# Top-2 gate dispatch: the first 14-row store waits for the landing of a 30-row load

## The chip, the cores and the metric

One core of one Trainium2 chip runs the kernel. The time is device microseconds of one execution, given as the median of several. The kernel before takes 240.29 us (three runs, 240.19 to 240.34).

## The reference

`x` holds 16 x 1024 tokens of 512 float32 values, `router_logits` 8 logits for each token, and k is 2.

```python
probs = softmax(router_logits)                      # over the 8 experts
topk_indices = np.argsort(probs, axis=-1)[..., -k:]
topk_probs = np.take_along_axis(probs, topk_indices, axis=-1)
topk_probs = topk_probs / np.sum(topk_probs, axis=-1, keepdims=True)
x_expanded = x[:, :, np.newaxis, :].repeat(k, axis=2)
return (x_expanded * topk_probs[..., np.newaxis]).astype(np.float32)
```

So each token is written out twice, scaled by the smaller and by the larger of its two normalized top-2 weights. With two weights the softmax cancels: they are the sigmoid of minus and plus the difference of the two largest logits. The kernel reads 33.6 MB of `x`, half a MB of logits, and writes 67.1 MB.

## The kernel before

**Layout.** The 16,384 tokens are dealt out in two groups (`GROUPS`, line 49): 128 partitions times 65 tokens, then 128 times 63. A "row" below is one token in each of the 128 partitions: 256 KB to load, 512 KB to store. `xs` holds the input rows of one group (65 rows), `osp` 16 rows of output. Within a partition the rows of one load or store are contiguous in HBM, so a load of 32 rows moves 128 pieces of 64 KB.

**Loads.** The loop at line 111 issues the loads of a group on SP's queue in the sizes of `LOADS` (line 51): 2, 4, 2, 8, 17 and 32 rows for the first group, 16, 16 and 31 for the second. After the second load the two loads of logits are issued (lines 116 and 117), and `top2_weights` finds the two largest logits of each token in a tournament on VectorE (lines 27 to 40), and on ScalarE two sigmoids (lines 42 and 43), which give `WA`.

**Products and stores.** `plan` (lines 120 to 126) lists the stretches of a group in order: first row, number of rows, place of the output. For the first group: 2 rows and 14 rows into `osp`; 16 rows into `xs[0:32]`, over input rows already used; 8 and 8 rows into the two halves of `osp`; then 9 and 8 rows over `xs[31:65]`. For the second group: 16 rows into `osp`, 16 over `xs`, 8 and 8 into `osp`, 15 over `xs`. `over` (line 98) finds the place in `xs`. For each stretch one multiplication on VectorE (line 128) writes both scaled copies, and one store follows (line 136), on ACT's queue for the 2-row stretch (`n == e`) and on SP's for all others.

**Order.** There is one core and no hand-written schedule: each engine takes its instructions in program order, and waits on semaphores where a tile is still to be read or written. SP issues all loads of the first group, then its stores, then the loads of the second group, each when the rows of `xs` it overwrites have been stored, then the stores of the second group. A store into `osp` must have landed before VectorE writes that part of `osp` again. Transfers complete on eight semaphores used in turn, and an issue that takes a semaphore again waits for the transfer that used it before.

The change touches the list of sizes (line 51), the loop of loads (lines 110 to 113) and the store (lines 135 and 136). The store it makes wait is the one with `g == 0` and `r == e`, which is the first group's second stretch: 14 rows from `osp`, 7168 KB, the first store on SP's queue.

Of the kernel before, what the change touches and what calls it, by code (L numbers as in the profile page):

```python
# [1 line left out]

# [4 lines left out]

F32 = mybir.dt.float32
ALU = mybir.AluOpType
ACTF = mybir.ActivationFunctionType  # L10
P = 128


def top2_weights(nc, pool, logits, M, E, tag=""):

    hi, lo, n = None, None, E  # L20
    while n > 1:
        n //= 2
        if hi is None:
            a, b = logits[:, :, 0:n], logits[:, :, n : 2 * n]
            nhi = pool.tile([P, M, n], F32, tag=f"hi{n}{tag}")
            nlo = b
            nc.vector.tensor_tensor(nhi, a, b, op=ALU.max)  # L27
            nc.vector.tensor_tensor(nlo, a, b, op=ALU.min)  # L28
        else:
            a, b = hi[:, :, 0:n], hi[:, :, n : 2 * n]  # L30
            nhi = pool.tile([P, M, n], F32, tag=f"hi{n}{tag}")
            nlo = pool.tile([P, M, n], F32, tag=f"lo{n}{tag}")
            tmp = pool.tile([P, M, n], F32, tag=f"tmp{n}{tag}")
            nc.vector.tensor_tensor(tmp, lo[:, :, 0:n], lo[:, :, n : 2 * n], op=ALU.max)  # L34
            nc.vector.tensor_tensor(nlo, a, b, op=ALU.min)  # L35
            nc.vector.tensor_tensor(nlo, nlo, tmp, op=ALU.max)  # L36
            nc.vector.tensor_tensor(nhi, a, b, op=ALU.max)  # L37
        hi, lo = nhi, nlo
    dlt = pool.tile([P, M], F32, tag=f"dlt{tag}")
    nc.vector.tensor_tensor(dlt, hi[:, :, 0], lo[:, :, 0], op=ALU.subtract)  # L40
    WA = pool.tile([P, M, 2], F32, tag=f"WA{tag}")
    nc.scalar.activation(WA[:, :, 0], dlt, ACTF.Sigmoid, scale=-1.0)  # L42
    nc.scalar.activation(WA[:, :, 1], dlt, ACTF.Sigmoid, scale=1.0)  # L43
    return WA

GROUPS = [65, 63]

LOADS = [[2, 4, 2, 8, 17, 32], [16, 16, 31]]


LAST = [[(48, 9), (57, 8)], [(48, 15)]]


@with_exitstack
def kernel(
    ctx: ExitStack,
    tc: tile.TileContext,  # L60
    x: bass.AP,
    router_logits: bass.AP,
    k: bass.AP,
    out: bass.AP,
):
    nc = tc.nc
    B, S, D = x.shape
    E = router_logits.shape[-1]
    N = B * S
    assert int(k) == 2 and E == 8 and N == P * sum(GROUPS)  # L70
    M = N // P

    L = 16
    x_v, o_v, rl_v = [], [], []
    t0 = 0
    for n in GROUPS:
        t1 = t0 + P * n
        x_v.append(
            x.rearrange("b s d -> (b s) d")[t0:t1].rearrange("(p m) d -> p m d", p=P)
        )  # L80
        o_v.append(
            out.rearrange("b s k d -> (b s) k d")[t0:t1].rearrange(
                "(p m) k d -> p m k d", p=P
            )
        )
        rl_v.append(
            router_logits.rearrange("b s e -> (b s) e")[t0:t1].rearrange(
                "(p m) e -> p m e", p=P
            )
        )  # L90
        t0 = t1

    wpool = ctx.enter_context(tc.tile_pool(name="wpool", bufs=1))
    logits = wpool.tile([P, M, E], F32)
    xs = wpool.tile([P, max(GROUPS), D], F32)
    osp = wpool.tile([P, L, 2, D], F32)

    def over(r, n, G):

        a = 2 * r - G
        return xs[:, a : a + 2 * n, :].rearrange("p (r k) d -> p r k d", k=2)

    h = L // 2
    e = 2
    m0 = 0
    for g, G in enumerate(GROUPS):
        r = 0  # L110
        for n in LOADS[g]:
            nc.sync.dma_start(xs[:, r : r + n, :], x_v[g][:, r : r + n, :])  # L112
            r += n
            if g == 0 and r == 6:

                nc.sync.dma_start(logits[:, :G], rl_v[0])  # L116
                nc.sync.dma_start(logits[:, G:], rl_v[1])
                WA = top2_weights(nc, wpool, logits, M, E)
        assert r == G
        begin = [(0, e, osp[:, :e]), (e, L - e, osp[:, e:])] if g == 0 else [(0, L, osp)]  # L120
        plan = begin + [
            (L, L, over(L, L, 2 * L)),
            (2 * L, h, osp[:, :h]),
            (2 * L + h, h, osp[:, h:]),
        ]
        plan += [(r, n, over(r, n, G)) for r, n in LAST[g]]
        for r, n, og in plan:
            nc.vector.tensor_tensor(  # L128
                og,
                xs[:, r : r + n, :].unsqueeze(2).to_broadcast([P, n, 2, D]),  # L130
                WA[:, m0 + r : m0 + r + n, :].unsqueeze(3).to_broadcast([P, n, 2, D]),
                op=ALU.mult,
            )

            queue = nc.scalar if n == e else nc.sync
            queue.dma_start(o_v[g][:, r : r + n], og)  # L136
        m0 += G


# [1 line left out]
_INS = ['x', 'router_logits', 'k']  # L141
_OUTS = [((16, 1024, 2, 512), 'float32')]

_NUMBERS = {'k': 2}


# [26 lines left out]
```

## Time and profile before

| what | us |
|---|---|
| median of three runs | 240.29 |
| span of the profiled execution, first to last instruction | 238.5 |
| VectorE busy | 142.0 |
| ScalarE busy | 1.8 |

SP's issues and VectorE's products, from the timeline (the start, then the length; a transfer's length here is that of the issue alone):

| start us | engine | what |
|---|---|---|
| 0.73 to 4.8 | SP | loads of 2, 4 rows, logits, loads of 2, 8, 17, 32 rows |
| 12.75 to 30.06 | VectorE | products of 2 and 14 rows |
| 15.08 | ACT | store of 2 rows |
| 30.07 | SP | store of 14 rows |
| 30.08 to 47.32 | VectorE | product of 16 rows, over `xs` |
| 47.33 | SP | store of 16 rows |
| 64.02 | VectorE | products of 8 and 8 rows, after 16.71 us of waiting |
| 102.30, 113.52, 123.48 | SP | loads of the second group |
| 214.42 | SP | last store |

The page's times are of one execution under the profiler. "q1" is SP's queue of transfers and "q10" ACT's; both are served by 16 DMA engines. A row of the view by windows gives the stretch, its length, the busy time of DVE, ACT and POOL in it with the number of instructions, the granted TensorE clock, the busy share of the DMA engines and their rate in GB/s. A landing time counts from the issue of a transfer to its completion. A strip of 40 numbers gives the rate in 40 equal slices, each packet booked in the slice in which it starts.

### The profile page before, as it was taken

To read this page: it belongs to the slowest core of one execution; us is meant where nothing else is said; L and a number is where in the kernel's file an instruction comes from. 1 tells how busy PE (TensorE), PEld (TensorE's weight loads), DVE (VectorE), ACT (ScalarE), POOL (GpSimd) and SP (SyncE) were. 2 spreads that over 40 slices of the span, in tenths; PEclk is the share of its full clock that TensorE was granted. 3 is DMA by queue.
4 is the path that set the end of the run, shared out by engine and by line. 5 is a ranking of instruction groups with operands and counts; after the bars stand their busy time and mean duration, and the time that the engine had idled before them with its cause. 6 is when DMAs were issued, how large, how long until landed. Compare 5 with 4: busy or idle time off the path is not lost.

```text
span 238.5 us, 116 instructions
## 1 busy us (share of the span) xinstructions
DVE 142.0 (60%) x23; ACT 1.8 (1%) x3; POOL 0.2 (0%) x4
## 2 busy tenths in 40 slices
DVE  0599999900299699900000699999006999990000
ACT  2000000000000000000000000000000000000000
POOL 0000000000000000000000000000000000000000
DMA  7999989899898999999999999998999989999994
GB/s 261 434 470 411 459 383 528 330 462 462 352 506 352 440 440 440 440 414 465 440 429 434 412 478 458 394 495 374 462 418 429 451 363 429 440 440 429 495 453 206
DMA packets 3312, 101.19 MB, mean 424 GB/s; under 512 B 368, under 2 KB 496, under 8 KB 880
## 3 DMA queue, kind: packets, MB, share of 16 engines
q1 hardware_dynamic: 3168, 100.14, 97.8%
q10 hardware_dynamic: 144, 1.05, 1.0%
HBM read 34.08 MB, written 67.11 MB: 424 GB/s over the span
## 4 chain that ended last, share of the span: by engine, by line
DMA 43%; DVE 41%; issue 4%; SPq 1%; ACT 0%; DVEq 0%
DVE xs L128 22%; DVE osp L128 18%; DMA out_dram<-xs 15%; DMA xs<-in_x_dram 13%; DMA out_dram<-osp 13%; DMA logits<-in_router_logits_dram 3%; SPq L112 0%; DVE nhi L27 0%; DVE logits L28 0%; DVE nlo L36 0%; DVE nhi L37 0%; DVE tmp L34 0%; DVE nlo L35 0%; SPq L116 0%; SPq L136 0%
## 5 line engine op out<-in xcount | busy, mean ns | idle before, releaser
L128 DVE TENSOR_TENSOR osp<-xs,WA 128x8192 f32<-128x8192 f32 (+3 forms) x7 | 69.1, 9908 | 61.9 <-DMA xs<-in_x_dram 31.2
L128 DVE TENSOR_TENSOR xs<-xs,WA 128x16384 f32<-128x16384 f32 (+3 forms) x5 | 69.1, 13812 | 2.2 <-DMA out_dram<-xs 2.0
L27 DVE TENSOR_TENSOR nhi<-logits 128x512 f32<-128x512 f32 x1 | 0.7, 691 | 8.3 <-DMA logits<-in_router_logits_dram 8.3
L42 ACT ACT_TABLE_LOAD x1 | 1.3, 1283 | 0.7 <-PEq L154 0.7
L28 DVE TENSOR_TENSOR logits<-logits 128x512 f32<-128x512 f32 x1 | 0.7, 692 | 0.0
L37 DVE TENSOR_TENSOR nhi<-nhi 128x256 f32<-128x256 f32 (+1 forms) x2 | 0.7, 351 | 0.0
L35 DVE TENSOR_TENSOR nlo<-nhi 128x256 f32<-128x256 f32 (+1 forms) x2 | 0.7, 350 | 0.0
L36 DVE TENSOR_TENSOR nlo<-nlo,tmp 128x256 f32<-128x256 f32 (+1 forms) x2 | 0.7, 350 | 0.0
L34 DVE TENSOR_TENSOR tmp<-logits 128x256 f32<-128x256 f32 x1 | 0.4, 418 | 0.0
L42 ACT ACTIVATE WA<-dlt 128x128 f32<-128x128 f32 x1 | 0.3, 315 | 10.2 <-DVE dlt L40 10.2
L40 DVE TENSOR_TENSOR dlt<-nhi,nlo 128x128 f32<-128x128 f32 x1 | 0.3, 291 | 0.0
L43 ACT ACTIVATE WA<-dlt 128x128 f32<-128x128 f32 x1 | 0.3, 297 | 0.0
L34 DVE TENSOR_TENSOR tmp<-nlo 128x128 f32<-128x128 f32 x1 | 0.3, 283 | 0.0
L154 POOL MEMSET const-bfloat16-1.0<- 128x1 bf16 x1 | 0.1, 101 | 0.0
L154 POOL MEMSET const-uint8-127<- 128x1 uint8 x1 | 0.1, 101 | 0.0
L154 POOL MEMSET const-float32-0.0<- 128x1 f32 x1 | 0.1, 98 | 0.2 <-issue 0.2
L154 POOL MEMSET const-float32-1.0<- 128x1 f32 x1 | 0.1, 98 | 0.0
## 6 DMA issues: line engine op xcount, KB each, us to landing
out_dram<-osp SPq DMA_DIRECT2D x4, 4096.0 KB, 20.7
xs<-in_x_dram SPq DMA_DIRECT2D x2, 4096.0 KB, 29.9
xs<-in_x_dram SPq DMA_DIRECT2D x1, 7936.0 KB, 38.0
out_dram<-xs SPq DMA_DIRECT2D x1, 7680.0 KB, 23.2
out_dram<-osp SPq DMA_DIRECT2D x1, 7168.0 KB, 33.9
out_dram<-xs SPq DMA_DIRECT2D x1, 4608.0 KB, 20.4
xs<-in_x_dram SPq DMA_DIRECT2D x1, 4352.0 KB, 22.4
out_dram<-xs SPq DMA_DIRECT2D x1, 4096.0 KB, 21.5
```

The lines of the kernel that those rows point to most:

```text
L27: nc.vector.tensor_tensor(nhi, a, b, op=ALU.max)
L28: nc.vector.tensor_tensor(nlo, a, b, op=ALU.min)
L34: nc.vector.tensor_tensor(tmp, lo[:, :, 0:n], lo[:, :, n : 2 * n], op=ALU.max)
L35: nc.vector.tensor_tensor(nlo, a, b, op=ALU.min)
L36: nc.vector.tensor_tensor(nlo, nlo, tmp, op=ALU.max)
L37: nc.vector.tensor_tensor(nhi, a, b, op=ALU.max)
L40: nc.vector.tensor_tensor(dlt, hi[:, :, 0], lo[:, :, 0], op=ALU.subtract)
L42: nc.scalar.activation(WA[:, :, 0], dlt, ACTF.Sigmoid, scale=-1.0)
L43: nc.scalar.activation(WA[:, :, 1], dlt, ACTF.Sigmoid, scale=1.0)
L128: nc.vector.tensor_tensor(og, xs[:, r : r + n, :].unsqueeze(2).to_broadcast([P, n, 2, D]), WA[:, m0 + r : m0 + r + n, :].unsqueeze(3).to_b ...
L154: nc = _bacc.Bacc("TRN2", target_bir_lowering=False, num_devices=1)
```

## The change

The first group's load of 32 rows is issued as two, of 30 rows and 2 rows. Loads and stores are kept in program order, and the first group's store of 14 rows gets a dependency on the second-last load, the one of 30 rows: SP issues it only once that load has landed, as well as the product of its rows. At that time only the load of 2 rows is ahead of it in the queue. SP's order of issue is otherwise the same; the computation and all other transfers are the same.

```diff
-LOADS = [[2, 4, 2, 8, 17, 32], [16, 16, 31]]
+LOADS = [[2, 4, 2, 8, 17, 30, 2], [16, 16, 31]]
...
-        r = 0
+        r, loads = 0, []
         for n in LOADS[g]:
-            nc.sync.dma_start(xs[:, r : r + n, :], x_v[g][:, r : r + n, :])
+            load = nc.sync.dma_start(xs[:, r : r + n, :], x_v[g][:, r : r + n, :])
+            loads.append(tc.keep_in_program_order(load))
             r += n
...
             queue = nc.scalar if n == e else nc.sync
-            queue.dma_start(o_v[g][:, r : r + n], og)
+            store = tc.keep_in_program_order(queue.dma_start(o_v[g][:, r : r + n], og))
+            if g == 0 and r == e:
+
+                tc.add_manual_dep(
+                    store.ins,
+                    loads[-2].ins.name,
+                    mybir.DependencyInfo(
+                        mybir.DependencyClass.Sync, mybir.DependencyReason.DATA
+                    ),
+                    reason="store behind the loads",
+                )
```

## The prediction

> **What bounds the kernel now.** I read the page first: is any engine or transfer the limit over the whole span? The answer is the transfers.
>
> ```profile
> span 238.5 us, 116 instructions
> DVE 142.0 (60%) x23; ACT 1.8 (1%) x3; POOL 0.2 (0%) x4
> q1 hardware_dynamic: 3168, 100.14, 97.8%
> HBM read 34.08 MB, written 67.11 MB: 424 GB/s over the span
> ```
>
> Packets of SP's queue alone (q1) fill 97.8% of the time of 16 DMA engines; VectorE (DVE) works 60%. So the chain of waits, which names DVE for 41%, only passes through work that lies beside transfers. A change pays, or costs, what it takes from or adds to the time in which the DMA engines stand still or run slowly. I therefore cut the span at the places where the kind of transfer changes, and read the rate of each stretch (the last column, GB/s; the column before is the busy share of the DMA engines).
>
> ```profile
> 0.00:1.74 1.74, 0.00 (x0) 1.01 (x1) 0.20 (x4) 1.00 0.00 0
> 1.74:4.00 2.26, 0.00 (x0) 0.27 (x1) 0.00 (x0) 1.00 1.02 330
> 33.56:43.22 9.66, 9.66 (x1) 0.00 (x0) 0.00 (x0) 1.00 1.00 434
> 43.22:46.19 2.97, 2.97 (x1) 0.00 (x0) 0.00 (x0) 1.00 1.03 353
> 46.19:63.10 16.91, 1.12 (x1) 0.00 (x0) 0.00 (x0) 1.00 1.00 434
> 63.10:82.42 19.32, 17.29 (x2) 0.00 (x0) 0.00 (x0) 1.00 1.00 434
> 82.42:112.67 30.25, 18.45 (x2) 0.00 (x0) 0.00 (x0) 1.00 1.00 433
> 112.67:141.71 29.04, 8.68 (x1) 0.00 (x0) 0.00 (x0) 1.00 1.00 433
> 141.71:160.44 18.73, 18.70 (x2) 0.00 (x0) 0.00 (x0) 1.00 1.01 434
> 160.44:218.44 58.00, 40.52 (x4) 0.00 (x0) 0.00 (x0) 1.00 1.00 434
> 218.44:236.56 18.12, 0.00 (x0) 0.00 (x0) 0.00 (x0) 1.00 1.00 434
> ```
>
> From 46.19 us to the end every stretch runs at 433 to 434 GB/s. So there is no slack behind the changed store: whatever it is late by is late at the end, one for one. One stretch is slow: 43.22 to 46.19 us, where the last eighth of the 32-row load goes through and the first big store begins. Slices of 0.1 us from 43 to 47 us show the starts of these packets:
>
> ```profile
> GB/s 0 0 4588 1966 2621 1311 0 0 0 0 0 0 0 0 0 0 0 0 0 0 0 0 0 0 0 0 0 0 0 0 0 573 1147 2294 2294 1720 1147 0 0 0
> ```
>
> A packet is booked where it starts. The last wave of the load starts between 43.2 and 43.6, the first wave of the store between 46.2 and 46.7 (the earliest at 46.19): 2.97 apart, where four earlier waves took 9.66 us, 2.42 each. The junction from load to store costs 0.55 us. The next such junction, at 160.44, shows nothing (434).
>
> Two more views give the instants of the issues and landings:
>
> ```profile
> 30.07 0.35 SPq L136 DMA_DIRECT2D out_dram<-osp  x1
> 47.33 0.34 SPq L136 DMA_DIRECT2D out_dram<-xs  x1
> ...
> xs<-in_x_dram SPq DMA_DIRECT2D x1, 42.6
> out_dram<-osp SPq DMA_DIRECT2D x1, 7168.0 KB, 33.9
> ```
>
> The store of 14 rows is issued at 30.07, 16 us before its first packet: it sits in the queue behind the load. The 32-row load is issued at 4.4 (two issues of 0.45 and 0.41 us from 3.85), so it lands at 47.0, 0.35 us after its last packet gives way to the store's.
>
> **The change, part by part.**
>
> *Two loads for one.* The bytes stay. One issue more on SP (0.4 us) falls before 8 us, when SP has nothing to issue until 30.07: hidden; uncovered it would cost its 0.4. It also waits for the landing of the 4-row load (the same semaphore is reused), at 6.9, long before its own bytes are due near 44.8. The short rows go in packets of 4 KB; the stretch 4.00 to 8.00, full of packets of 2 to 8 KB, still ran at 405 GB/s, so 0.52 MB cost 1.29 instead of 1.21 us: +0.08, beside the wait below, so 0 in the sum and +0.08 where the wait vanishes.
>
> *The wait.* Without the slow junction the 32 rows would end at 45.6 to 46.0 (43.2 to 43.6 plus 2.42). Two rows are 1.21 us at 433 GB/s, so the 30-row load ends at 44.4 to 44.8 and lands at 45.15 (plus the 0.35 above). SP then issues; take 0.05, since the second group's second load was issued at 113.52 when the 4608 KB store whose rows it overwrites landed (93.15 + 20.4 = 113.55): no delay to be seen. From issue to the first packet: the row is the kernel's first load, issued at 0.73, nothing moving before 1.74, its 16 first packets starting from 1.74 to 2.05: 1.01 to 1.32. So the store starts at 46.2 to 46.5, middle 46.36; before it was 46.2 to 46.7, middle 46.45. Difference -0.09.
>
> *The refill.* After an emptied queue the rate is not full at once: 1.74 to 4.00 moved 0.746 MB, which is 1.72 us at 433, in 2.26. Of the 0.54 lost, 0.15 is the mean of the spread of starts, counted already; 0.39 is the upper bound (those were small reads from HBM, this is a large write), 0 the lower. I take half, +0.2.
>
> *Sum:* 238.5 - 0.09 + 0.2 = 238.6 of span; the median 240.29 lies 1.8 above the profiled span, which stays: 240.4.
>
> *What the wait holds back.* Behind the store on SP is the 16-row store, which needs DVE until 47.33; the wait ends at about 45.2, so 2.1 us of cover are left; only an issue after 47.33 would move it. ACT and DVE wait for nothing new: DVE's next product (64.02) waits for the same store's landing and moves with it. Its cover further on is ample: at 214.42 the last store is issued 4 us before its packets are due at 218.44.
>
> *Bounds of the unknown.* The time from issue to first packet behind two moving rows has no row of its own. Least: 0.35, the issue instruction itself (then the two rows' end decides). Most: the 2-row store on ACT's queue was issued at 15.08, and the queue's first packets stand in the stretch from 18 to 19 us,
>
> ```profile
> q10 hardware_dynamic: 7, 0.06, 13.5%
> ```
>
> from about 18.6 on: 3.5 us after the issue, among long packets of the other queue. I take 1.01, the row of the same queue with nothing ahead; the two small rows are nearer to that than to a queue with packets of 34 KB.
>
> A rule of the Trainium skill speaks against the change (DMA: Bandwidth & Descriptors, "Anatomy of one DMA"): any wait happens on the issuing sequencer, engines just consume what is queued, and each DMA has about 2 us fixed, mostly the confirmation of the last byte. By that figure 2.0 less the 1.21 of the two rows would be a gap of 0.8, and after the 0.55 of the junction +0.25: 240.5. The trace's own 0.35 and 1.01 make 1.4.
>
> **Rivals.**
>
> *Faster: the store follows the two rows without a gap and the slow junction is gone.* Gain 0.55 less 0.08: -0.47, 239.8. For it: the load lands 1.2 us before the queue is empty. Against: it needs 0.5 us or less from issue to packet, half of what the one clean row has. Even this is the whole of it, because nothing else in the trace is slow after 46.19.
>
> *Slower: the junction's 0.55 belongs to the first big store on SP's queue, not to its having been queued behind a load.* Then it is paid after the gap as well: +0.11 + 0.55 = +0.66, 240.95. For it: the second junction, load to store in the same manner, cost nothing, so queueing alone does not make it. Against: the stretched packets are the load's, not the store's. It decides if the time from issue to first packet is 1.5 us or more, or if the store's first wave is longer than 2.1 us.
>
> *Slower: generation of the packets is late beside moving data,* towards ACT's row: halfway between 1.01 and 3.54 is 2.28, +1.27 on the forecast, 241.7; it decides above 1.4 us.
>
> *The change does nothing:* the load would have to land before 30.07; the 42.6 us exclude it.
>
> **How the numbers follow.** What a measurement of this kernel tells from no change is about 0.2%, 0.48 us. Forecast 240.4, its own range 240.05 to 240.75 (the refill from 0 to 0.39, 0.15 for the landing): 47%. Faster rival 13%, of which half may reach past 239.8 by some relief I don't see. First-store rival 22%, late generation 18%. So faster 0.13, same 0.47, slower 0.40. The range takes in the faster rival's time and the lower half of late generation: 239.7 to 241.5.
>
> **What would show it.** In the changed profile: the 30-row load lands at 45.0 to 45.4; SP's first big store is issued within 0.1 us of that; no packet starts for some 0.3 to 0.6 us before the store's first wave at 46.2 to 46.6; the last wave of the 30-row load lasts 2.27, not 2.8. If the DVE product that began at 64.02 begins at 64.0 to 64.3, the sum holds; at 63.6 the faster rival is right, from 64.6 on a slower one. The prediction is wrong, too, if later stretches drop below 433 GB/s, that is, if the order on the 16 DMA engines matters beyond this junction.

## The result, and the profile after

The changed kernel takes 241.98 us (five runs, 241.97 to 242.1) against 240.29: a ratio of 1.0069, 95% interval 1.0057 to 1.008. It is 0.7% slower; 240.4 was forecast, in a range up to 241.5.

The page after, in the same lines as before: the engines do the same work, the bytes are the same, and the span has grown by 1.8 us.

```profile
span 240.3 us, 116 instructions
DVE 142.0 (59%) x23; ACT 1.8 (1%) x3; POOL 0.2 (0%) x4
q1 hardware_dynamic: 3312, 100.14, 97.7%
HBM read 34.08 MB, written 67.11 MB: 421 GB/s over the span
```

Did the wait do what was said? SP's issues and landing times, and the starts of packets in slices of 0.1 us from 43 to 47 us:

```profile
45.36 0.35 SPq L137 DMA_DIRECT2D out_dram<-osp  x1
47.40 0.34 SPq L137 DMA_DIRECT2D out_dram<-xs  x1
...
xs<-in_x_dram SPq DMA_DIRECT2D x1, 7680.0 KB, 40.9
out_dram<-osp SPq DMA_DIRECT2D x1, 7168.0 KB, 18.3
...
GB/s 0 0 0 0 0 0 0 0 0 0 0 0 0 0 205 164 410 451 328 532 410 369 451 410 369 532 246 246 82 41 0 0 6881 2294 0 0 0 0 0 0
```

It did. The load of 30 rows lands at 45.3 (issued at 4.44), the store is issued at 45.36 instead of 30.07, the two small rows run from 44.4 to 46.0, two slices are empty, and the first packets of the store stand in two slices, 46.2 to 46.4, where before they were spread over six. No packet is stretched at this junction any more. The next product on VectorE begins earlier than before, at 63.78 instead of 64.02. But the lines after it, VectorE's products of the changed kernel, tell of a loss:

```profile
63.78 17.29 DVE L129 TENSOR_TENSOR osp<-xs,WA 128x8192 f32<-128x8192 f32 x2 [16.40 <-DMA out_dram<-osp]
83.21 18.48 DVE L129 TENSOR_TENSOR xs<-xs,WA 128x9216 f32<-128x9216 f32 x2 [2.14 <-DMA out_dram<-xs]
134.00 17.23 DVE L129 TENSOR_TENSOR osp<-xs,WA 128x16384 f32<-128x16384 f32 x1 [32.30 <-DMA xs<-in_x_dram]
```

Before, these began at 64.02, 83.36 and 133.03: the changed kernel is 0.24 ahead, then 0.15 ahead, then 0.97 behind. By its last store (issued at 216.33 instead of 214.42) it is 1.9 behind. The windows of the changed kernel, cut where waves of packets begin (a wave is one packet on each of the 16 engines), show where:

```profile
44.44:46.21 1.77, 1.77 (x1) 0.00 (x0) 0.00 (x0) 1.00 0.74 296
46.21:63.21 17.00, 1.17 (x1) 0.00 (x0) 0.00 (x0) 1.00 1.02 439
63.21:82.59 19.38, 17.29 (x2) 0.00 (x0) 0.00 (x0) 1.00 0.99 426
82.59:112.98 30.39, 18.45 (x2) 0.00 (x0) 0.00 (x0) 1.00 1.00 431
...
121.50:123.29 1.79, 0.00 (x0) 0.00 (x0) 0.00 (x0) 1.00 0.96 256
...
159.12:162.42 3.30, 3.30 (x1) 0.00 (x0) 0.00 (x0) 1.00 1.06 328
162.42:220.41 57.99, 39.52 (x4) 0.00 (x0) 0.00 (x0) 1.00 1.00 433
```

Two views of the kernel before, for comparison: the starts of packets from 118 to 126 us, where the waves follow each other every 1.2 us, and the window of the load wave near 160 us.

```profile
GB/s 0 0 0 492 983 1147 0 0 0 492 819 1311 0 0 0 328 983 1311 0 0 0 328 983 1147 164 0 0 328 819 1147 328 0 0 328 819 1147 328 0 0 328
...
158.08:160.44 2.36, 2.36 (x1) 0.00 (x0) 0.00 (x0) 1.00 1.03 430
```

The three store windows up to 112.98 and that of 159.12 hold the same packets as their counterparts in the kernel before, so lengths can be compared. The three store stretches up to 112.98 take 17.00, 19.38 and 30.39 instead of 16.91, 19.32 and 30.25: 0.3 us more in all. Then two windows stand out, and they are the two places where the queue changes direction: 121.50 to 123.29, the last wave of the first group's stores, with loads queued behind it (256 GB/s; a wave took 1.2 before), and 159.12 to 162.42, the last wave of the second group's loads, with stores queued behind it (328 GB/s; the same wave took 2.36 before).

I call these places J1 (load to store, near 46 us), J2 (store to load, near 122) and J3 (load to store, near 160). The tables below give for each the mean lengthening of the packets of the last wave against undisturbed ones, per DMA engine, worked out from the packet records of each trace. For the two kernels:

| kernel | J1 | J2 | J3 |
|---|---|---|---|
| before | 0.66 | 0.00 | 0.08 |
| changed | waited away | 0.85 | 1.01 |

The account of the changed kernel, by the mean over the engines: the store's first packets come 0.16 earlier, the store waves up to J2 lose 0.3, J2 0.85, J3 0.93 more than before: +1.9, where the span shows 1.8.

### The profile page after: what moved, and what is told of

Its sections match the earlier page's. It is cut to its first block, busy times and chain, and to the rows that moved or that the text cites. A ratio compares the mean times of both kernels' runs of the same rounds, so it can differ in the third digit from the quotient of the medians.

```text
span 240.3 us, 116 instructions
## 1 busy us (share of the span) xinstructions
DVE 142.0 (59%) x23; ACT 1.8 (1%) x3; POOL 0.2 (0%) x4
## 4 chain that ended last, share of the span: by engine, by line
DMA 44%; DVE 41%; issue 4%; SPq 1%; ACT 0%; DVEq 0%
DVE xs L129 22%; DVE osp L129 18%; DMA out_dram<-xs 15%; DMA xs<-in_x_dram 13%; DMA out_dram<-osp 13%; DMA logits<-in_router_logits_dram 3%; SPq L112 0%; DVE nhi L27 0%; DVE logits L28 0%; DVE nlo L36 0%; DVE tmp L34 0%; DVE nhi L37 0%; DVE nlo L35 0%; SPq L117 0%; SPq L137 0%
```

## The experiments

Each run was compared with the kernel before, run beside it.

**The split without the wait.** The dependency is left out, the sizes 30 and 2 stay.

```diff
-            if g == 0 and r == e:
+            if False:
```

> The 30+2 split stays, the wait is gone. Three theories. Lockstep: the wait empties the queue, all 16 DMA engines restart within 0.15 us, and the two later changes of direction (store to load near 122 us, load to store near 160 us) pay for it with 0.8 and 1.0 us; without the wait the engines keep their old spread (0.45 us), so the time is that of the kernel before, 240.3 +-0.3, with the slow junction near 46 us still there. Split: the added transfer shifts what comes after; the later junctions stay slow, 241.9 or more. Late issue: a junction is slow where the store is queued early; the first junction is as before, 240.3.

Measured: 240.23 us, ratio 0.9992 (0.9976 to 1.0008). J1 0.49, J2 0.03, J3 0.14. The second load costs nothing; the split theory falls.

**The wait without the split.** The store waits for a load of 32 rows, with nothing behind it.

```diff
-LOADS = [[2, 4, 2, 8, 17, 30, 2], [16, 16, 31]]
+LOADS = [[2, 4, 2, 8, 17, 32], [16, 16, 31]]
...
-                    loads[-2].ins.name,
+                    loads[-1].ins.name,
```

> The wait stays, on the unsplit 32-row load: nothing covers the wait. Lockstep: the queue is dry for 1.4 us (0.35 landing, 1.01 to the first packet) from 45.6-46.0, so the store starts near 47.1 (+0.7 against before, +0.8 against the changed kernel), and the later junctions are slow as in the changed kernel: 242.8. Split: the gap alone, 241.0, later junctions as before.

Measured: 243.32 us, ratio 1.0123 (1.0108 to 1.0138). J2 0.87, J3 0.98: as dear as in the changed kernel. The windows of this run show the dry queue, 1.8 us without the start of a packet; by the packet records the earliest engine stood idle that long, the last one, done at 46.15, for 1.35:

```profile
45.70:47.49 1.79, 1.78 (x1) 0.00 (x0) 0.00 (x0) 1.00 0.00 0
```

So the two rows of the changed kernel do cover 1.3 us (243.32 against 241.98), and the loss behind is not theirs.

**More cover: 24+8, 28+4 and 26+6.** Only the sizes differ from the changed kernel; the wait is on the second-last load.

```diff
-LOADS = [[2, 4, 2, 8, 17, 30, 2], [16, 16, 31]]
+LOADS = [[2, 4, 2, 8, 17, 24, 8], [16, 16, 31]]
```

> Split 24+8, the wait on the 24 rows: the load lands near 41.5 and the store is issued with 8 rows (4.8 us) ahead of it, so the queue is never empty. Lockstep: no restart, so 240.3 +-0.3, first junction slow (0.5), later ones cheap. Split: 242. Late issue: the first junction's 0.55 shrinks if it comes from the store having lain 16 us in the queue: 239.8.

> Split 28+4, the wait on the 28 rows: landing near 43.9, first packet ready by 45.2, the 4 rows end at 45.6-46.1: the queue just stays full. Lockstep: 240.3 as in the 24+8 run, later junctions cheap. Split: 242. If what matters is only that the store is issued late, it goes with the changed kernel: first junction free, later ones slow, 242.

> Between 24+8 (240.25) and 28+4 (242.6). The store's packets are ready near 43.8, 1.8 us before the load's end. If a lead of 2 us or less is what makes the later junctions dear: 242. If it is any lead that the engines can see in time: first junction slow (0.5), later ones cheap, 240.3; a mixture of the two in one kernel's executions would say that the switch lies here.

| split | store issued | J1 | J2 | J3 | us | ratio |
|---|---|---|---|---|---|---|
| 24+8 | 41.87 | 0.48 | 0.01 | 0.06 | 240.25 | 0.9997 (0.9987 to 1.0007) |
| 26+6 | 43.01 | 0.03 | 0.18 | 0.66 | 241.44 | 1.0046 (1.0032 to 1.0061) |
| 28+4 | 44.29 | 0.02 | 0.76 | 0.69 | 242.59 | 1.0077 (1.0056 to 1.0099) |

With 26+6 and 28+4 the queue is never empty (by the packet records each engine goes straight from its last load to the store), and yet J3, and with 28+4 J2 as well, is dear where J1 was free. My theory that the engines must have been brought into step by an empty queue is too narrow. The 28+4 kernel also scatters (240.78 to 243.04 over nine executions), which no other kernel here does so widely. A store queued 3.8 us ahead of the loads' end (some 45.7) gives the old picture whole; one queued 2.7 us ahead or less takes J1's cost away and brings later ones.

**A restart between two stores.** The kernel before, in which the first group's 16-row store waits for the landing of its 14-row store. No change of direction is touched. The edit is shown against the changed kernel.

```diff
-LOADS = [[2, 4, 2, 8, 17, 30, 2], [16, 16, 31]]
+LOADS = [[2, 4, 2, 8, 17, 32], [16, 16, 31]]
...
+            stores.append(store)
-            if g == 0 and r == e:
+            if g == 0 and r == L:
...
-                    loads[-2].ins.name,
+                    stores[-2].ins.name,
```

> No split and no wait at the first store; instead the 16-row store behind it waits for the landing of the 14-row store, so the queue runs dry between two stores (0.35 + 1.01 = 1.4 us). Restart order: what makes the later junctions dear is that the 16 engines leave a dry queue in the order of their issue; the first junction is slow as before (+0.6), and the junctions near 122 and 160 us cost 0.8 and 1.0 besides the gap: 243.3. Late first store: what makes them dear is that the first store was queued less than some 2 us ahead of the load's end, so they stay cheap here and the gap alone is paid: 241.7.

Measured: 243.88 us, ratio 1.015 (1.0134 to 1.0165). J1 0.56 as before; J2 0.88, J3 0.81. Windows of this run: the last wave at J1, the gap, and the waves at J2 and J3.

```profile
43.21:46.15 2.94, 2.94 (x1) 0.00 (x0) 0.00 (x0) 1.00 1.01 357
...
63.06:65.16 2.10, 0.82 (x1) 0.00 (x0) 0.00 (x0) 1.00 0.08 31
...
123.50:125.28 1.78, 0.00 (x0) 0.00 (x0) 0.00 (x0) 1.00 0.94 258
...
161.24:164.21 2.97, 2.97 (x1) 0.00 (x0) 0.00 (x0) 1.00 1.11 364
```

An emptied queue is enough to make J2 and J3 dear, 58 and 96 us later, with the first store queued early and J1 paid. A late first store is not needed.

**A restart between two loads.** The second group's load of 31 rows waits for the landing of the load before it.

```diff
+            if g == 1 and n == 31:
+                tc.add_manual_dep(load.ins, loads[-2].ins.name, ...)
```

> Nothing is changed at the first store; the second group's load of 31 rows waits for the landing of the load of 16 rows before it, so the queue runs dry once between two loads near 142 us (about 1.5 us, as in the run with the restart between stores). Restart makes later junctions dear: the junction near 46 us slow and the one near 122 cheap, as before, and the one near 160 us costs 1.0: 242.8. Restart does it only among stores: 241.8.

Measured: 244.24 us, ratio 1.0164 (1.0147 to 1.0181). J2, which lies ahead of the restart, 0.03; J3, behind it, 1.24. Windows: the gap, the first wave after it, the wave at J3.

```profile
141.70:143.83 2.13, 2.13 (x1) 0.00 (x0) 0.00 (x0) 1.00 0.00 0
143.83:146.79 2.96, 2.96 (x1) 0.00 (x0) 0.00 (x0) 1.00 1.12 365
...
160.93:164.31 3.38, 3.38 (x1) 0.00 (x0) 0.00 (x0) 1.00 1.06 301
```

The sum expected for it was 1.4 short: the gap is longer than the 1.5 taken for it, the first wave of loads after it is slow too (2.96 for 2.34), and J3 is dearer than in the changed kernel. That first wave is a cost of restarted loads which the restarted stores didn't have (2.15 for 2.12 in the changed kernel).

**A restart with no junction behind it.** The second group's second store waits for the landing of its first.

> The second group's second store waits for the landing of its first, near 181 us; no change of direction lies behind it. Restart makes later junctions dear: there is none, so only the gap is paid, 240.3 + 1.5 = 241.8. If a restarted queue is slower all along (as the store waves of 2.42 to 2.43 instead of 2.418 us hint): up to 0.3 more, 242.1.

Measured: 242.15 us, ratio 1.0087 (1.0057 to 1.0117). J1 0.57, J2 0.01, J3 0.09, all as in the kernel before. What is paid is the gap:

```profile
158.09:160.48 2.39, 2.39 (x1) 0.00 (x0) 0.00 (x0) 1.00 1.02 425
...
179.80:181.84 2.04, 0.87 (x1) 0.00 (x0) 0.00 (x0) 1.00 0.00 0
```

The same restart costs 3.6 us near 64 (243.88 against 240.27) and 1.9 us near 181 (242.15 against 240.23). The difference, 1.7, is about what J2 and J3 cost in the first of the two (0.88 and 0.81).

**The same trick at J3 as well.** The changed kernel, and the second group's last load split into 29 and 2, its first store waiting for the 29.

```diff
-LOADS = [[2, 4, 2, 8, 17, 30, 2], [16, 16, 31]]
+LOADS = [[2, 4, 2, 8, 17, 30, 2], [16, 16, 29, 2]]
...
-            if g == 0 and r == e:
+            if r == (e if g == 0 else 0) and not (g == 0 and n == e):
```

> The changed kernel, and the same trick at the second group: its load of 31 rows split into 29 and 2, its first store waiting for the 29. If the wait takes the junction's cost away wherever it stands, the 1.0 near 160 us goes and the 0.8 near 122 us stays: 241.0. If it only pushes the cost to the next change of direction, there is none behind it: also 241.0. If the gap costs as much as the junction: 242.

Measured: 241.74 us, ratio 1.0061 (1.0045 to 1.0078). J2 0.85 as in the changed kernel; the stretch at J3 is gone, but only 0.24 of its 1.0 is gained: the waited start costs 0.6 of it (from the two rows' first packets at 160.28 to the store's at 162.10, 1.82 us for 1.2 us of bytes). The expectation of 241.0 was wrong in that.

**Are the engines too close together?** After the restart the 16 engines start within 0.15 us; before, within 0.45. Three runs shift some of them by small loads of 4 KB per partition into the used-up `logits` tile, behind the 14-row store. In the first, 8 partitions once; in the second, 8 partitions four times; in the third, 8, 4, 2 and 1 partitions. The edit of the second:

```diff
+                for c in range(4):
+                    tc.keep_in_program_order(
+                        nc.sync.dma_start(
+                            logits[8 * c : 8 * c + 8].rearrange("p m e -> p (m e)"),
+                            x_v[1][8 * c : 8 * c + 8, :2, :].rearrange("p m d -> p (m d)"),
+                        )
+                    )
```

> The changed kernel, and behind the 14-row store a load of 4 KB into each of 8 partitions of the used-up logits tile (32 KB more, on 8 of the 16 engines, 0.16 us each). Restart order: it sets half of the engines back behind the others, the order after the restart is gone, and the junctions near 122 and 160 us lose a good part of their 1.7: 240.5 to 241.3. Late first store: nothing changes but the 0.16: 242.1.

> As the run that set half of the engines back by 0.16 us, with four such loads: 0.64 us. Phase of the two halves: if engines of the two halves must not change direction at the same time, 0.64 parts them and the junctions near 122 and 160 us become cheap; the kernel pays the 0.64 and saves most of 1.7: 241.0. If the restart's order within the halves, or anything else, is what counts: 242.0 + 0.6 = 242.6.

> The changed kernel, and behind its 14-row store four small loads of 4 KB per partition into 8, 4, 2 and 1 partitions of the used-up logits tile: they set 1, 1, 2 and 4 of the engines back by 0.64, 0.48, 0.32 and 0.16 us. Spread theory (the engines that leave a dry queue within 0.15 us of each other change direction together, and that is dear): a spread of 0.7 us as in the kernel before makes the junctions near 122 and 160 us cheap, the worst engine pays 0.64: 240.9 to 241.3. Spread is not what counts: 242.0 + 0.5 = 242.5, the junctions as dear as in the run with half of the engines set back by 0.64 (0.6 and 0.7).

| shift as planned | J2 | J3 | us | ratio |
|---|---|---|---|---|
| 8 engines, 0.16 us | 0.89 | 0.96 | 242.1 | 1.0074 (1.0059 to 1.0089) |
| 8 engines, 0.64 us | 0.60 | 0.66 | 242.45 | 1.0089 (1.0073 to 1.0104) |
| 1, 1, 2 and 4 engines, 0.64 to 0.16 us | 0.84 | 0.97 | 244.35 | 1.0168 (1.0151 to 1.0185) |

In the second run both junctions fall by a third, no more. By the packet records the two halves stand 0.9 us apart there, not 0.64, and the fall at J2 lies in the half that carries the small loads: its packets are lengthened by 0.39, those of the other half by 0.76. These engines have also been through an early change of direction (store, load, store), which a run below shows to spare J2, so this run doesn't tell whether it is the shift or that change that helps. The staircase lowers nothing on average. It makes the whole spread at J2 0.89 us wide, but twelve engines still start within 0.12 us, so it says little on a narrow spread. (The staircase's time is that of its slowest engine, which starts its last wave of loads 1.0 us behind the others.)

The 28+4 run says more: its engines start the last store wave over 0.56 us, where the kernel before has 0.45, and J2 costs 0.76 all the same. A narrow spread isn't needed for a dear junction.

**The shift without the restart.** The kernel before, with the four small loads of 8 partitions.

> The kernel before, no wait and no split, with the four small loads (8 partitions each) behind its 14-row store: half of the engines set back by 0.64 us, but no restart. If the cheap junctions near 122 and 160 us hang on one fragile phase of the engines, the shift breaks it: 240.3 + 0.64 + 1 or more, 242. If they hang on whether the queue has been restarted since its last slow change of direction: they stay cheap, 240.3 + 0.64 = 240.9.

Measured: 241.28 us, ratio 1.0038 (1.0025 to 1.0051). J1 0.58, J2 0.05, J3 0.52. J2 stays free under a shift of 0.64, so it does not hang on a fine phase; J3 does not stay free. Neither expectation holds whole.

**An early change of direction.** The changed kernel, and a load of 4 KB into all 128 partitions of `logits` behind the 14-row store: the restarted engines go from store to load to store near 63 us.

```diff
+                tc.keep_in_program_order(
+                    nc.sync.dma_start(
+                        logits.rearrange("p m e -> p (m e)"),
+                        x_v[1][:, :2, :].rearrange("p m d -> p (m d)"),
+                    )
+                )
```

> The changed kernel, and behind its 14-row store a load of 4 KB into all 128 partitions of the used-up logits tile (512 KB, 1.25 us): the restarted engines change direction twice near 63 us, store to load to store. If the first change of direction after a restart spreads the engines so that the later ones are cheap (as the slow first junction seems to do in the kernel before): 242.0 + 1.25 + 0.8 - 1.7 = 242.3. If each change stays dear: 242.0 + 1.25 + 1.6 = 244.8.

Measured: 242.88 us, ratio 1.0106 (1.0089 to 1.0123), with 1.25 us more bytes. The two early changes together cost 0.95 (0.78 in the store's last wave, 0.17 in the small loads); J2 is then 0.16 instead of 0.85, J3 0.62 instead of 1.01. Windows: the last wave of the 14-row store, then the wave at J2.

```profile
61.04:63.73 2.69, 0.00 (x0) 0.00 (x0) 0.00 (x0) 1.00 1.08 341
...
123.31:124.69 1.38, 0.00 (x0) 0.00 (x0) 0.00 (x0) 1.00 0.99 380
```

That is nearer to the 242.3 of a change that spares the later ones than to 244.8: with a dear change of direction early on, most of J2 and part of J3 become free.

**What the runs show together.** A change of direction on SP's queue with the next transfer already queued costs each engine 0.5 to 1.2 us where it is the first after the start of the kernel or after a restart of the queue (J1 before, J2 after the changed kernel's wait, J3 after the restart in loads, the early one near 63). After a slow J1 without a restart J2 is free in all six runs that have it so (before, split alone, 24+8, restart in loads, late restart, shifted half), and J3 nearly so (0.14 or less) in those that reach it without a restart or a shift. The 26+6 and 28+4 runs fit this less well: J1 is free in them without a restart, J2 costs 0.18 in the one and 0.76 in the other, J3 0.66 and 0.69. The changed kernel has both things that go with dear later junctions, a J1 that isn't paid and a queue that nearly runs dry; the runs show that either does it without the other (28+4; the restart between two stores), not which one acts in it. What a slow change alters in the engines is not shown: a narrow spread isn't needed, the shift of one half explains a third at most, and after the dear J2 of the changed kernel its J3 is dear all the same.

No version tried beats the kernel before; the split alone (0.9992) and 24+8 (0.9997) are equal to it.

## Why the prediction was wrong, by its own steps

- *What bounds the kernel:* right. The loss is all in the rate of transfers; VectorE's 142.0 us did not change and nothing hid the loss.
- *The two loads for one at nothing:* right (the split alone, 240.23).
- *The wait's sum:* right in its result. Forecast for the landing 45.15, issue within 0.1, first packets 46.2 to 46.5; seen 45.3, 45.36, 46.2 to 46.4. Two terms were off by some 0.15 and cancelled, which is luck: the landing came later, 0.46 after the last packet's end instead of 0.35, and the first packet followed the issue by 0.85 instead of 1.01. The junction's 0.55 did vanish; in its place came a gap of 0.38 per engine (by the packet records the two rows end at 45.89 on average, the store's packets start at 46.27).
- *The refill of 0.2:* too high; the store's first wave took 2.15 for 2.12, the whole stretch 17.00 for 16.91. The product behind it began at 63.78 instead of 64.0 to 64.3, on the fast side of the forecast: it waits for the last engine, whose first packet came at 46.35 instead of 46.65.
- *The step that failed:* "whatever it is late by is late at the end, one for one", drawn from "from 46.19 us to the end every stretch runs at 433 to 434 GB/s". The rates behind the junction were read as a property of these stretches. They were a property of this course of the queue: after the wait, the same stretches lose 0.3 in the stores, 0.85 at J2 and 0.93 at J3. At 64 us the forecast was kept and bettered, at the end it was missed by 1.6.
- *A sign that was there:* the profile had two load-to-store junctions, one slow and one free. I used this for the first-store rival, against queueing as the cause, and then took the free one for granted. A cost that stands at one of two like places has a condition, and I did not ask whether the edit touches it.
- *The rivals:* none had this mechanism. The first-store rival's 240.95 and late generation's 241.7 are nearer in time, but their signs are absent: issue to packet took 0.85, not 1.4 or more. The other sign of the first-store rival, a first wave longer than 2.1 us, was badly set: the wave took 2.15, but it took 2.12 in the kernel before too. That the side, slower, had 0.40 is luck as far as the mechanism goes.
- *The rule on the fixed cost (the Trainium skill, DMA: Bandwidth & Descriptors, "Anatomy of one DMA"):* the section describes transfers that GpSimd issues, and here SP issues them, which the prediction doesn't say. As a pause between a load and the store that waits for it, its 2 us are too much here. In the changed kernel the last engine ended the 30 rows at 44.83 and the first packet of the store came at 46.21, 1.38 later; with the uncovered wait it was 1.35. The 1.4 summed from rows of the trace was right.
- *The last sentence of the prediction* named the sign that came: wrong "if later stretches drop below 433 GB/s". It put that down to the order on the 16 DMA engines, which no run shows, and gave it no chance and no price.

## What to carry to other kernels

Where a kernel is bound by 16 DMA engines that never stop, an edit that lets the queue run dry, or nearly, must be judged by all changes between loads and stores behind it, not by the junction it mends; compare the landing times along the whole span, since a gain seen at 64 us was a loss at 134. A stretch at full rate in the old profile is no promise that it stays so. Queue the next direction's transfer well ahead (here 3.8 us kept the old picture, 2.7 did not), and pay the one slow change.

## What the runs showed of the hardware

- A change of direction of a full queue lengthens the last packets before it, by 0.5 to 1.2 us per engine, or by 0.2 or less, depending on what the queue went through up to 100 us earlier (0.88 and 0.81 at J2 and J3, 58 and 96 us behind the restart between two stores; 0.00 and 0.08 without it).
- Restarted stores run in a narrow front (starts within 0.15 us) and slightly slower, 0.4% (75.3 us from the changed kernel's first store packet, 46.21, to its last store wave, 121.50; 74.95 before).
- In the changed kernel the half of the engines that started first took 2.1 to 2.3 us for the wave at J2, the other half 1.7 to 1.9 (one each the other way). With eight engines set back by 0.16 us it was nearly all of the later half that took 2.1 to 2.4. That reads as if the same half paid more, whichever leads; the records do not name the engines, so it is not shown.
- A wait on a landing with nothing queued behind it left 1.8 to 2.1 us in which no packet started (the wait without the split and the three restarts), though the last engine was idle for only 1.25 to 1.35 of it: the rest is the spread of the ends.
